# A fixed order for the fp32 weighted sums of grouped heads, and scores against both parts of the keys in one product

## The chip, the cores and the metric

The kernel runs on one core of a Trainium2 chip. The metric is the device time of one execution in microseconds (us), as the median of several runs. TensorE (PE, with its weight loads PEld) multiplies, VectorE (DVE) and ScalarE (ACT) work elementwise, GpSimd (POOL) and SyncE (SP) mostly issue transfers.

## The reference

A decoder trunk of four layers on x of 256 rows by 2048, in fp32. The layers use three kinds of self attention in turn: latent (layers 0 and 3), sparse grouped with a top-k selection of keys (layer 1), and grouped with a sliding window and sinks (layer 2). Every layer also has four memory heads of width 256, which attend to 256 memory rows.

```
h   = rmsnorm(x) ;  q, k, v, mq, gate = split(h @ w_in[i])
s   = q k^T * scale + bias ; masked ; p = softmax(s) ; self = p v      # 32 heads, 4 key groups
sm  = mq mk^T / 16         ;          pm = softmax(sm) ; mem = pm mv   # 4 memory heads
x   = x + (concat(self, mem) * silu(gate)) @ w_out[i]
```

The grouped layers have 32 heads of width 64; eight heads share one of four groups of keys and values. After the last layer a final rmsnorm is applied.

## The kernel before

Matrices are multiplied in fp32r. An fp32 operand is split into a high part (rounded by ACT, line 74) and a low part (the difference, by DVE, line 83), and a product is made of high by high, high by low and low by high. Weights stream from memory through `wr` (SP's queue), are split into `wh` and `wl`, and are multiplied at lines 289 (`rows_by`, output and value weights), 310 and 314 (`columns_by`, queries and gates).

The program is written layer by layer: for each of six parts of a layer (two of memory heads, four of self heads), project, attend, gate, and then the output weights of the part before. A scheduler that simulates the program then places the instructions on each engine, each engine's queue running in order, so that the attention of one part stands among the weight products of others. `tc.keep_in_program_order` pins an instruction behind the pinned ones before it on its engine.

The attention of a grouped layer is `Grouped.attend`, once per group `g` of keys. Its outer loop runs over two halves, the inner one over `odd` in (0, 1), two sets of two heads, 64 queries at a time. For each, `quarter_softmax` takes two of four query quarters `r`; the keys up to the quarter's end count, (r + 1) * 64, or 192 for the last quarter of the windowed layer.

- Scores (line 1033): the queries' high and low parts lie on the 128 partitions, so one product of n keys' high and low parts side by side gives both halves of the score, 2n columns. For the sparse layer's last quarter (n = 256) there are instead two products of 256 columns into the same place (line 1036). `both(r)` tells the two apart.
- Where both halves come apart, DVE adds the bias to the low one (line 601), then adds the high one and takes the minimum (line 603); otherwise line 603 alone adds the bias. ACT takes the exponential (line 605) and normalizes it (line 74).
- PE transposes the weights into `ptp` (line 550), and ACT copies them to `pT`, one tile for each `odd`, in fp32.
- Weighted sums (line 1065): four fp32 products make `o` of 128 partitions by 512 columns. `odd` 0 fills partitions 0 to 63 and uses the array's columns 0 to 63, `odd` 1 the others. For each, keys 0 to 127 (t = 0) give 512 columns and keys 128 to 255 (t = 1) add to the last 256. Their weights are the values, 128 keys by 64. The hardware runs an fp32 product as two passes, which the trace records as two products.
- DVE multiplies `o` by the gate (line 1070), and the result is split into `y` for the output weights.

`memory_attend` does the same for two memory heads of 256. With `both` (layers 0 and 3), lines 652 and 653 make the scores of 128 queries with two products of 512 columns (high queries by both parts of the keys) and two of 256 (low queries by high keys); ACT copies the second half out and DVE adds it while taking the minimum (line 656). Without (layers 1 and 2), line 663 uses six products of 256 columns, and DVE takes the maximum of the sum (line 664).

Of the kernel before, what the change touches and what calls it, by code (L numbers as in the profile page):

```python
# [8 lines left out]
F32 = mybir.dt.float32  # L9
F32R = mybir.dt.float32r  # L10
I32 = mybir.dt.int32
AF = mybir.ActivationFunctionType
OP = mybir.AluOpType
# [32 lines left out]
def kernel(ctx: ExitStack, tc: tile.TileContext, a: dict, out: bass.AP,  # L46
# [536 lines left out]
            normalized(es[b], r[:, b:b + 1], (b + 1) * P)  # L583
        return weights_T(es, [(0, 0), (1, 0), (1, 1)])

    def quarter_softmax(score, bias, first_key, both, b, nsk):

        es = []
        mn, sm = small("mn", 2), small("sm", 2)
        for i, r in enumerate((2 * b, 2 * b + 1)):  # L590
            k0, k1 = first_key(r), (r + 1) * 64
            n = k1 - k0
            sp = score(r, k0, n)
            u = wk.tile([P, S], F32, name="u", tag="e", bufs=4)
            e = wk.tile([P, S], F32, name="e", tag="e", bufs=4) if nsk is None else u
            for z0, z1 in ((0, k0), (k1, (b + 1) * P)):
                if z0 < z1:
                    nc.gpsimd.memset(e[:, z0:z1], 0.0)
            bi, at = bias(r, k0, k1), u[:, k0:k1]
            if both(r):  # L600
                nc.vector.tensor_add(at, sp[:, n:2 * n], bi)
                bi = at
            nc.vector.tensor_tensor_reduce(at, sp[:, :n], bi, -1.0, nsk if nsk is not None else BIG,
                                           op0=OP.add, op1=OP.min, accum_out=mn[:, i:i + 1])
            nc.scalar.activation(e[:, k0:k1], at, AF.Exp, bias=mn[:, i:i + 1], scale=-1.0,
                                 accum_out=sm[:, i:i + 1])
            es.append((e, k0, k1))
        rc = small("rc", 2)
        if nsk is not None:
            d = small("sd", 2)  # L610
            nc.vector.tensor_scalar(d, mn, nsk, None, op0=OP.subtract)
            e2 = small("se", 2)
            nc.scalar.activation(e2, d, AF.Exp)
            s3 = small("sa", 2)
            nc.vector.tensor_add(s3, sm, e2)
            nc.vector.reciprocal(rc, s3)
        else:
            nc.vector.reciprocal(rc, sm)
        for i, (e, k0, k1) in enumerate(es):
            copy_act(e[:, k0:k1], e[:, k0:k1], scale=rc[:, i:i + 1])  # L620
        return weights_T([e for e, _, _ in es], [(i, k) for k in range(b + 1) for i in range(2)])
# [17 lines left out]
            qT.append(q)  # L639
        return nm, kT, v, qT, gate(nm, w, g0 + 2048 + part * 512)  # L640

    def memory_attend(both, nm, kT, v, qT, gT):
        y = act.tile([P, 2, 4, S], F32R, name="y", tag="y", bufs=2)
        for h in range(2):
            es = []
            mn, sm = small("mn", 2), small("sm", 2)
            for b in range(2):
                sp = misc("msp")
                qs = slice(b * P, (b + 1) * P)
                if both:  # L650
                    for k in range(2):
                        nc.tensor.matmul(sp, qT[h][:, 0, k, qs], kT[h][:, :, k, :], start=k == 0, stop=False)
                        nc.tensor.matmul(sp[:, :S], qT[h][:, 1, k, qs], kT[h][:, 0, k, :], start=False, stop=k == 1)
                    s = wk.tile([P, S], F32, name="u", tag="e", bufs=4)
                    copy_act(s, sp[:, S:])
                    nc.vector.tensor_tensor_reduce(s, sp[:, :S], s, -1.0, BIG,
                                                   op0=OP.add, op1=OP.min, accum_out=mn[:, b:b + 1])
                    factor = "neg"
                else:
                    seq = [(qT[h][:, u, k, qs], kT[h][:, v_, k, :])  # L660
                           for k in range(2) for u, v_ in ((0, 0), (0, 1), (1, 0))]
                    for n_, (l, r_) in enumerate(seq):
                        nc.tensor.matmul(sp[:, :S], l, r_, start=n_ == 0, stop=n_ == len(seq) - 1)
                    nc.vector.tensor_reduce(mn[:, b:b + 1], sp[:, :S], AX.X, OP.max, negate=True)
                    s, factor = sp[:, :S], "rstd"
                ms = small("ms", 2)
                nc.vector.tensor_mul(ms[:, :1], mn[:, b:b + 1], nm.col("rstd", b))
                e = wk.tile([P, S], F32, name="e", tag="e", bufs=4)
                nc.scalar.activation(e, s, AF.Exp, bias=ms[:, :1], scale=nm.col(factor, b),
                                     accum_out=sm[:, b:b + 1])  # L670
                es.append(e)
            r = small("rc", 2)
            nc.vector.reciprocal(r, sm)
            for b in range(2):
                normalized(es[b], r[:, b:b + 1], S)
            tp = weights_T(es, [(0, 0), (1, 0), (0, 1), (1, 1)])
            pH, pL = (wk.tile([P, 768], F32R, name="pT", tag="pT", bufs=PT)[:, :512] for z in range(2))
            split(pH, pL, tp)
            o = misc("mo")
            for j in range(2):  # L680
                c = (2 * h + j) * P
                seq = [(v[z][:, t, c:c + P], p_[:, t * S:(t + 1) * S])
                       for t in range(2) for z, p_ in ((0, pH), (0, pL), (1, pH))]
                for n_, (l, r_) in enumerate(seq):
                    nc.tensor.matmul(o[:, j * S:(j + 1) * S], l, r_, start=n_ == 0, stop=n_ == 5)
            gated(y, o, gT, 2 * h)
        return y
# [169 lines left out]
    class Grouped:  # L857
# [164 lines left out]
        def attend(self, g, q, bm, gT):  # L1022
# [3 lines left out]
            for half in range(2):  # L1026
                pT = []
                for odd in range(2):
                    def score(r, k0, n):
                        sp = misc("sp")  # L1030
                        qb = q[half][:, odd, r].rearrange("p j c -> p (j c)")
                        if both(r):
                            nc.tensor.matmul(sp[:, :2 * n], qb, self.k[:, g, :, k0:k0 + n], start=True, stop=True)
                        else:
                            for v in range(2):
                                nc.tensor.matmul(sp[:, :n], qb, self.k[:, g, v, k0:k0 + n],
                                                 start=v == 0, stop=v == 1)
                        return sp

                    def bias(r, k0, k1):  # L1040
                        c0 = (3 - r) * 64
                        bh = bm[:, half * 2 + odd, c0 + k0:c0 + k1]
                        if not self.sparse or r == 0:
                            return bh
                        bs = wk.tile([P, S], F32, name="bs", tag="e", bufs=4)[:, :k1]
                        nc.vector.tensor_add(bs, bh, self.sel[r])
                        return bs

                    def first_key(r):
                        return 64 if r == 3 and not self.sparse else 0  # L1050

                    def both(r):
                        return r < 3 or not self.sparse

                    u0 = g * 4 + half * 2 + odd
                    nsk = None if self.sparse else nsink[:, u0:u0 + 1]
                    pT.append(wk.tile([P, 6, P], F32, name="pT2", tag="pT", bufs=PT))
                    for b in range(2):
                        tp = quarter_softmax(score, bias, first_key, both, b, nsk)
                        i0, i1 = ((0, 2), (2, 6))[b]  # L1060
                        copy_act(pT[odd][:, i0:i1], tp[:, :(i1 - i0) * P].rearrange("p (i c) -> p i c", c=P))
                o = misc("o")
                for t in range(2):
                    for odd in range(2):
                        nc.tensor.matmul(o[64 * odd:64 * odd + 64, t * S:], self.v[:, t, g * 64:g * 64 + 64],
                                         pT[odd][:, 4 * t:4 + 2 * t].rearrange("p i c -> p (i c)"),
                                         start=t == 0, stop=t == 1, tile_position=(0, 64 * odd))
                j = half * 2
                yt = tmp("yt")
                nc.vector.tensor_mul(yt.rearrange("p (j r c) -> p j r c", j=2, r=4),  # L1070
# [148 lines left out]
    for i in range(depth):  # L1219
# [20 lines left out]
        order = [4, 0, 1, 2, 3, 5]  # L1240
        for n_, part in enumerate(order):
            if part >= 4:
                y = memory_attend(kind == 0, *memory_project(nm, i, mixer.w, mixer.mq0, mixer.g0, part - 4,
                                                  mixer.last_of_first()))
            else:
                y = mixer.attend(*mixer.project(part))
            if pending is not None:
                w_out(*pending, False)
            pending = (part, y)
# [62 lines left out]
```

## Time and profile before

| | |
|---|---|
| median of 3 runs | 2571.69 us (2570.69 to 2571.88) |
| the profiled execution, time | 2570.63 us |
| its span, first to last instruction | 2568.9 us |
| granted TensorE clock, mean | 0.999 |
| weighted sums (line 1065), records on PE | 128 |
| scores of memory heads, layers 1 and 2 (line 663) | 96 products |
| the second form of the sparse scores (line 1036) | 32 products |

A row of groups reads: line, engine, operation, tile written and tiles read, shapes, count, then busy us in total and mean ns of one, then the engine's idle time before them and what ended it. A row of the timeline reads: start in us, length in us, engine, line, operation, count. PE's instructions overlap: the next one's start, and not the first one's end, tells when PE went on. A row of the waits says who waited for whom: us in total, times, longest.

### The profile page before, as it was taken

What the parts mean: (1) busy time and instruction counts of PE and PEld (TensorE: products, weight loads), DVE (VectorE), ACT (ScalarE), POOL (GpSimd) and SP (SyncE); (2) the same over time, 40 slices, a digit from 0 to 9 for tenths busy, and PEclk for the clock granted to TensorE, in tenths of its full rate; (3) what the DMA queues carried; (4) which work ended last, traced back from release to release, by engine and by line L of the source; (5) the groups of instructions that cost most, each with busy time, mean ns of one, the idle gap of its engine ahead of it and who ended that gap; (6) DMA issues with size and microseconds to landing.
All of it is one profiled execution on the core that took longest, in us unless ns stands there. A gap on an engine that the chain in (4) does not pass through costs nothing.

```text
span 2568.9 us, 41673 instructions
## 1 busy us (share of the span) xinstructions
PE 2558.5 (100%) x14022; PEld 2186.3 (85%) x14022; DVE 1885.3 (73%) x3800; ACT 1596.3 (62%) x3271; POOL 102.9 (4%) x297
## 2 busy tenths in 40 slices
PE   9999999999999999999999999999999999999998
PEld 8888898888888889888888888888888888888887
DVE  6666667677777687987777777777768767777766
ACT  6556556566566566666666566666656666666655
POOL 1200000000000000000000000000000000000000
PEclk9999999999999999999999999999999999999999
DMA  9888777576677667665666565565555768666765
GB/s 310 262 265 257 238 224 227 165 196 178 183 203 204 185 199 205 197 194 164 185 181 175 170 214 179 165 180 166 176 168 161 238 189 221 190 195 186 222 168 185
DMA packets 478583, 511.68 MB, mean 199 GB/s; under 512 B 70656, under 2 KB 391040, under 8 KB 477728
## 3 DMA queue, kind: packets, MB, share of 16 engines
q1 hardware_dynamic: 461856, 451.82, 59.9%
q0 software_dynamic: 15792, 56.22, 7.0%
q8 instruction: 110, 1.80, 0.3%
q14 instruction: 105, 0.86, 0.1%
q10 hardware_dynamic: 720, 0.98, 0.1%
HBM read 483.67 MB, written 29.46 MB: 200 GB/s over the span
## 4 chain that ended last, share of the span: by engine, by line
PE 98%; DMA 1%; DVE 1%; ACT 0%; issue 0%; SPq 0%; POOL 0%; ACTq 0%; DVEq 0%
PE acc_wo L289 20%; PE acc_g L310 14%; PE acc_g L314 7%; PE acc_mv L289 7%; PE acc_q L310 5%; PE acc_mk L310 5%; PE acc_mq L310 4%; PE acc_cq L310 3%; PE acc_qn L310 3%; PE acc_q L314 2%; PE acc_mk L314 2%; PE acc_mq L314 2%; PE acc_cq L314 2%; PE acc_qr L310 2%; PE acc_qn L314 2%; PE acc_va L289 2%
## 5 line engine op out<-in xcount | busy, mean ns | idle before, releaser
L83 DVE TENSOR_TENSOR wl<-wr,wh 128x512 fp32r<-128x512 f32 (+1 forms) x1712 | 1154.5, 679 | 581.1 <-ACT wh L74 551.5
L74 ACT ACTIVATE wh<-wr 128x512 fp32r<-128x512 f32 (+1 forms) x1712 | 1063.0, 623 | 830.9 <-PE acc_g L310 148.1
L310 PE MATMUL acc_g<-xT,wh 128*128 128x512 f32 x1536 | 483.4, 397 | 0.0
L289 PE MATMUL acc_wo<-wh,y 128*128 128x512 f32 x1504 | 477.1, 392 | 0.0
L289 PEld LDWEIGHTS acc_wo<-wh,y 128*128 128x128 f32 x1504 | 282.5, 188 | 58.9 <-ACT th L531 1.5
L314 PEld LDWEIGHTS acc_g<-xT,wl 128*128 128x128 f32 x1536 | 280.8, 188 | 60.6 <-DVE wl L83 0.5
L314 PE MATMUL acc_g<-xT,wl 128*128 128x256 f32 x1536 | 306.0, 281 | 0.1
L289 PE MATMUL acc_wo<-wl,y 128*128 128x512 f32 x752 | 297.7, 396 | 0.0
L310 PEld LDWEIGHTS acc_g<-xT,wh 128*128 128x128 f32 x1536 | 235.3, 189 | 0.8
L289 PEld LDWEIGHTS acc_wo<-wl,y 128*128 128x128 f32 x752 | 141.4, 188 | 25.9
L310 PE MATMUL acc_q<-xT,wh 128*128 128x512 f32 x512 | 161.3, 396 | 0.0
L310 PE MATMUL acc_mq<-xT,wh 128*128 128x512 f32 x512 | 161.1, 396 | 0.0
L310 PE MATMUL acc_mk<-mT,wh 128*128 128x512 f32 x512 | 160.7, 395 | 0.0
L289 PE MATMUL acc_mv<-wh,mT 128*128 128x512 f32 x512 | 156.8, 390 | 0.2
L310 PE MATMUL acc_qn<-cT,wh 128*128 128x512 f32 x384 | 121.0, 396 | 0.0
L310 PE MATMUL acc_cq<-xT,wh 128*128 128x512 f32 x384 | 120.9, 396 | 0.0
L1231 DVE TENSOR_TENSOR xc<-xc,acc_wo 128x1024 f32<-128x1024 f32 x92 | 112.0, 1218 | 4.2 <-PE acc_wo L289 3.4
L314 PEld LDWEIGHTS acc_mk<-mT,wl 128*128 128x128 f32 x512 | 95.8, 188 | 22.6 <-DVE wl L83 0.2
L289 PEld LDWEIGHTS acc_mv<-wh,mT 128*128 128x128 f32 x512 | 96.3, 188 | 20.7 <-ACT wh L74 0.9
L314 PEld LDWEIGHTS acc_q<-xT,wl 128*128 128x128 f32 x512 | 95.0, 188 | 21.5
L314 PEld LDWEIGHTS acc_mq<-xT,wl 128*128 128x128 f32 x512 | 94.5, 188 | 21.4 <-issue 0.4
L314 PE MATMUL acc_mq<-xT,wl 128*128 128x256 f32 x512 | 101.8, 280 | 0.0
(325 smaller groups left out, 3837.1 us busy)
## 6 DMA issues: line engine op xcount, KB each, us to landing
wr<-in_w_out_dram SPq DMA_DIRECT2D x188, 512.0 KB, 3.7
wr<-in_w_in_a_dram SPq DMA_DIRECT2D x176, 512.0 KB, 4.2
wr<-in_w_mem_kv_dram SPq DMA_DIRECT2D x126, 512.0 KB, 4.8
wr<-in_w_in_b_dram SPq DMA_DIRECT2D x116, 512.0 KB, 3.6
wr<-in_w_in_c_dram SPq DMA_DIRECT2D x104, 512.0 KB, 3.5
wr<-in_w_uq_dram SPq DMA_DIRECT2D x288, 128.0 KB, 2.8
wr<-in_w_in_a_dram SPq DMA_DIRECT2D x32, 288.0 KB, 3.1
mv<-mv POOLq DMA_DIRECT2D x16, 512.0 KB, 6.5
```

The source lines that it names most:

```text
L74: inst = nc.scalar.activation(o, i, AF.Copy, scale=scale)
L83: nc.vector.tensor_sub(lo, src, f32(hi))
L289: nc.tensor.matmul(acc[t][:, :n], q[:, v, (s + k) % 4, t * P:(t + 1) * P], w_[:, :n], start=s + k == 0 and v == 0 and w_ is wh, stop=s + k ...
L310: nc.tensor.matmul(acc[j], wh[:, o:o + P], q[:, :, kt % 4, :], start=kt == 0, stop=False)
L314: nc.tensor.matmul(acc[j][:, 0, :], wl[:, o:o + P], q[:, 0, kt % 4, :], start=False, stop=kt == kts - 1)
L1231: nc.vector.tensor_add(xs, xs, acc)
```

## The change

`quarter_softmax` and `memory_attend` lose their second form, and the four weighted sums of a half are pinned, `odd` 1 ahead of `odd` 0 for each t.

```diff
-            bi, at = bias(r, k0, k1), u[:, k0:k1]
-            if both(r):
-                nc.vector.tensor_add(at, sp[:, n:2 * n], bi)
-                bi = at
-            nc.vector.tensor_tensor_reduce(at, sp[:, :n], bi, -1.0, nsk if nsk is not None else BIG,
+            at = u[:, k0:k1]
+            nc.vector.tensor_add(at, sp[:, n:2 * n], bias(r, k0, k1))
+            nc.vector.tensor_tensor_reduce(at, sp[:, :n], at, -1.0, nsk if nsk is not None else BIG,
...
-                    seq = [(qT[h][:, u, k, qs], kT[h][:, v_, k, :])
-                           for k in range(2) for u, v_ in ((0, 0), (0, 1), (1, 0))]
-                    for n_, (l, r_) in enumerate(seq):
-                        nc.tensor.matmul(sp[:, :S], l, r_, start=n_ == 0, stop=n_ == len(seq) - 1)
-                    nc.vector.tensor_reduce(mn[:, b:b + 1], sp[:, :S], AX.X, OP.max, negate=True)
-                    s, factor = sp[:, :S], "rstd"
+                for k in range(2):
+                    nc.tensor.matmul(sp, qT[h][:, 0, k, qs], kT[h][:, :, k, :], start=k == 0, stop=False)
+                    nc.tensor.matmul(sp[:, :S], qT[h][:, 1, k, qs], kT[h][:, 0, k, :], start=False, stop=k == 1)
+                s = wk.tile([P, S], F32, name="u", tag="e", bufs=4)
+                copy_act(s, sp[:, S:])
+                nc.vector.tensor_tensor_reduce(s, sp[:, :S], s, -1.0, BIG,
...
-                        if both(r):
-                            nc.tensor.matmul(sp[:, :2 * n], qb, self.k[:, g, :, k0:k0 + n], start=True, stop=True)
-                        else:
-                            for v in range(2):
-                                nc.tensor.matmul(sp[:, :n], qb, self.k[:, g, v, k0:k0 + n],
-                                                 start=v == 0, stop=v == 1)
+                        nc.tensor.matmul(sp[:, :2 * n], qb, self.k[:, g, :, k0:k0 + n], start=True, stop=True)
...
                 for t in range(2):
-                    for odd in range(2):
-                        nc.tensor.matmul(o[64 * odd:64 * odd + 64, t * S:], self.v[:, t, g * 64:g * 64 + 64],
+                    for odd in (1, 0):
+                        tc.keep_in_program_order(
+                            nc.tensor.matmul(o[64 * odd:64 * odd + 64, t * S:], self.v[:, t, g * 64:g * 64 + 64],
```

Lines move up by 3 to 18 with it: the scores of memory heads are lines 649 and 650, the grouped scores line 1021, the weighted sums line 1047, and their multiplication by the gate line 1052.

The instructions also move. On PE, layer 1, the first group's first half, where `pT_12586` is the tile of `odd` 0 and `pT_12645` that of `odd` 1, there stands before:

```order
L550 MATMUL ptp<-ident,e 128x128
L1065 MATMUL o<-pT_12586,vs 64x512
L1033 MATMUL sp<-kd,qS 128x128
L1033 MATMUL sp<-kd,qS 128x256
L550 MATMUL ptp<-ident,e 128x128 x3
...
L289 MATMUL acc_wo<-wh,y 128x512
L1065 MATMUL o<-pT_12645,vs 64x512
L1065 MATMUL o<-pT_12586,vs 64x256
L1065 MATMUL o<-pT_12645,vs 64x256
L289 MATMUL acc_wo<-wh,y 128x512
```

and there after the change:

```order
L550 MATMUL ptp<-ident,e 128x128 x4
L289 MATMUL acc_wo<-wl,y 128x512
L289 MATMUL acc_wo<-wh,y 128x512 x2
...
L1047 MATMUL o<-pT_12645,vs 64x512
L1047 MATMUL o<-pT_12586,vs 64x512
L1047 MATMUL o<-pT_12645,vs 64x256
L1047 MATMUL o<-pT_12586,vs 64x256
L1021 MATMUL sp<-kd,qS 128x128
L1021 MATMUL sp<-kd,qS 128x256
```

The product of `odd` 0 with 512 columns has moved from between the transposes, 18 weight products ahead of the others, into one run with them, 12 weight products behind the last transposes. It is so in all 16 halves of the two layers: one product and a run of three before, a run of four now; before, the lone one was followed by scores in eight halves and by transposes in the other eight.

On PE, a little earlier, the first scores of the sparse layer's third and fourth quarters stood like this:

```order
L550 MATMUL ptp<-ident,e 128x128
L1033 MATMUL sp<-kd,qS 128x384
L1036 MATMUL sp<-kd,qS 128x256 x2
L314 MATMUL acc_g<-xT,wl 128x256 x2
L310 MATMUL acc_g<-xT,wh 128x512 x2
```

and now stand like this:

```order
L550 MATMUL ptp<-ident,e 128x128
L1021 MATMUL sp<-kd,qS 128x384
L314 MATMUL acc_g<-xT,wl 128x256 x2
L310 MATMUL acc_g<-xT,wh 128x512 x2
L314 MATMUL acc_g<-xT,wl 128x256 x2
L1021 MATMUL sp<-kd,qS 128x512
L550 MATMUL ptp<-ident,e 128x128
```

The two products of 256 have become one of 512, and some weight products have moved between the two quarters' scores. SP's queue keeps its order, and POOL's differs by where three fills with zeros stand.

More of the change, by code (lines that the diff above doesn't have):

```diff
@@ L584, in masked_softmax, with quarter_softmax @@
         return weights_T(es, [(0, 0), (1, 0), (1, 1)])
-    def quarter_softmax(score, bias, first_key, both, b, nsk):
+    def quarter_softmax(score, bias, first_key, b, nsk):
         es = []
@@ L640, in memory_project, with memory_attend @@
         return nm, kT, v, qT, gate(nm, w, g0 + 2048 + part * 512)
-    def memory_attend(both, nm, kT, v, qT, gT):
+    def memory_attend(nm, kT, v, qT, gT):
         y = act.tile([P, 2, 4, S], F32R, name="y", tag="y", bufs=2)
@@ L649, in memory_attend @@
                 qs = slice(b * P, (b + 1) * P)
[L650 to L658, printed above, removed]
-                else:
-                    seq = [(qT[h][:, u, k, qs], kT[h][:, v_, k, :])
-                           for k in range(2) for u, v_ in ((0, 0), (0, 1), (1, 0))]
-                    for n_, (l, r_) in enumerate(seq):
-                        nc.tensor.matmul(sp[:, :S], l, r_, start=n_ == 0, stop=n_ == len(seq) - 1)
-                    nc.vector.tensor_reduce(mn[:, b:b + 1], sp[:, :S], AX.X, OP.max, negate=True)
-                    s, factor = sp[:, :S], "rstd"
+                for k in range(2):
[4 more added lines that the diff above has]
+                nc.vector.tensor_tensor_reduce(s, sp[:, :S], s, -1.0, BIG,
+                                               op0=OP.add, op1=OP.min, accum_out=mn[:, b:b + 1])
                 ms = small("ms", 2)
@@ L668, in memory_attend @@
                 e = wk.tile([P, S], F32, name="e", tag="e", bufs=4)
-                nc.scalar.activation(e, s, AF.Exp, bias=ms[:, :1], scale=nm.col(factor, b),
+                nc.scalar.activation(e, s, AF.Exp, bias=ms[:, :1], scale=nm.col("neg", b),
                                      accum_out=sm[:, b:b + 1])
@@ L1031, in score @@
                         qb = q[half][:, odd, r].rearrange("p j c -> p (j c)")
-                        if both(r):
-                            nc.tensor.matmul(sp[:, :2 * n], qb, self.k[:, g, :, k0:k0 + n], start=True, stop=True)
-                        else:
-                            for v in range(2):
-                                nc.tensor.matmul(sp[:, :n], qb, self.k[:, g, v, k0:k0 + n],
-                                                 start=v == 0, stop=v == 1)
+                        nc.tensor.matmul(sp[:, :2 * n], qb, self.k[:, g, :, k0:k0 + n], start=True, stop=True)
                         return sp
@@ L1050, in first_key @@
                         return 64 if r == 3 and not self.sparse else 0
-                    def both(r):
-                        return r < 3 or not self.sparse
                     u0 = g * 4 + half * 2 + odd
@@ L1058, in attend @@
                     for b in range(2):
-                        tp = quarter_softmax(score, bias, first_key, both, b, nsk)
+                        tp = quarter_softmax(score, bias, first_key, b, nsk)
                         i0, i1 = ((0, 2), (2, 6))[b]
@@ L1063, in attend @@
                 for t in range(2):
-                    for odd in range(2):
-                        nc.tensor.matmul(o[64 * odd:64 * odd + 64, t * S:], self.v[:, t, g * 64:g * 64 + 64],
-                                         pT[odd][:, 4 * t:4 + 2 * t].rearrange("p i c -> p (i c)"),
-                                         start=t == 0, stop=t == 1, tile_position=(0, 64 * odd))
+                    for odd in (1, 0):
+                        tc.keep_in_program_order(
+                            nc.tensor.matmul(o[64 * odd:64 * odd + 64, t * S:], self.v[:, t, g * 64:g * 64 + 64],
+                                             pT[odd][:, 4 * t:4 + 2 * t].rearrange("p i c -> p (i c)"),
+                                             start=t == 0, stop=t == 1, tile_position=(0, 64 * odd)))
                 j = half * 2
@@ L1242 @@
             if part >= 4:
-                y = memory_attend(kind == 0, *memory_project(nm, i, mixer.w, mixer.mq0, mixer.g0, part - 4,
+                y = memory_attend(*memory_project(nm, i, mixer.w, mixer.mq0, mixer.g0, part - 4,
                                                   mixer.last_of_first()))
```

## The prediction

> **What bounds the kernel now.** I read the page of the profiled execution first: the busy times of part 1, then the chain that ended last in part 4.
>
> ```profile
> PE 2558.5 (100%) x14022; PEld 2186.3 (85%) x14022; DVE 1885.3 (73%) x3800; ACT 1596.3 (62%) x3271; POOL 102.9 (4%) x297
> ...
> PE 98%; DMA 1%; DVE 1%; ACT 0%; issue 0%; SPq 0%; POOL 0%; ACTq 0%; DVEq 0%
> ```
>
> TensorE (PE) is busy for 2558.5 of 2568.9 us, and 98% of the last chain is its own work. So the kernel costs what its products cost, one behind the other, unless PE is made to wait. The change touches layers 1 and 2 alone, so I looked next at a stretch of layer 1's attention (the windows view: busy time and count of each engine, then the granted clock), and at whom PE waited for in the whole program (the waits view: total us, times, longest).
>
> ```profile
> 1100.00:1400.00 300.00, 300.00 (x1594) 243.56 (x1593) 228.81 (x518) 200.96 (x452) 12.03 (x44) 1.00 0.61 179
> ```
>
> ```profile
> PE msp L663 <- DMA mkr<-mkT: 0.6, 1, 0.6
> ```
>
> In these 300 us PE is never free, at the full clock (1.00), while VectorE (DVE) has 71 us to spare and ScalarE (ACT) 99 us. Apart from the program's first product, the only wait that the view puts on PE is 0.6 us for a memory key tile. An edit is therefore worth what it does to PE's queue; work on the other engines is free as long as it comes in time.
>
> **The weighted sums.** A busy PE is made of overlapping durations here, so I don't use means of one instruction; I use the distance from one start to the next, which adds up to the span. The groups view says what the sums are: 32 products of 512 columns, each run as two passes (64 records), and as many of 256.
>
> ```profile
> L1065 PE MATMUL o<-pT,vs 128*64 128x512 f32 x64 | 34.3, 618 | 0.0
> ```
>
> In the order before, each of the 16 halves (2 layers, 4 groups, 2 halves) has one early product alone and a later run of three. The timeline of PE (start, length, line) shows an early one between a transpose and a pair of scores, and below it the same pair without it.
>
> ```profile
> 1123.22 0.27 PE L550 MATMUL ptp<-ident,e 128*128 128x128 f32 x1
> 1123.42 1.07 PE L1065 MATMUL o<-pT,vs 128*64 128x512 f32 x2
> 1124.42 0.50 PE L1033 MATMUL sp<-kd,qS 128*128 128x128 f32 x2
> 1124.76 0.49 PE L550 MATMUL ptp<-ident,e 128*128 128x128 f32 x3
> ```
>
> ```profile
> 1110.74 0.27 PE L550 MATMUL ptp<-ident,e 128*128 128x128 f32 x1
> 1110.77 0.48 PE L1033 MATMUL sp<-kd,qS 128*128 128x128 f32 x2
> 1111.09 0.49 PE L550 MATMUL ptp<-ident,e 128*128 128x128 f32 x3
> ```
>
> From the transpose to the next transposes it is 1.54 us with the early product (1124.76 - 1123.22) and 0.35 us without (1111.09 - 1110.74): it costs 1.19 us. Only 1.00 us lies between its own start and the next one's; the rest is the delay of the product before it and of the one behind it. In eight of the 16 halves the neighbours are scores as here; in the other eight a run of transposes is cut in two:
>
> ```profile
> 1153.38 0.27 PE L550 MATMUL ptp<-ident,e 128*128 128x128 f32 x1
> 1153.59 1.07 PE L1065 MATMUL o<-pT,vs 128*64 128x512 f32 x2
> 1154.59 0.55 PE L550 MATMUL ptp<-ident,e 128*128 128x128 f32 x3
> 1154.89 0.49 PE L314 MATMUL acc_q<-xT,wl 128*128 128x256 f32 x2
> ```
>
> ```profile
> 1087.06 0.60 PE L550 MATMUL ptp<-ident,e 128*128 128x128 f32 x4
> 1087.41 0.48 PE L314 MATMUL acc_q<-xT,wl 128*128 128x256 f32 x2
> ```
>
> That is 1.51 us against 0.35 us for four transposes in one run, so 1.16 us. Both kinds together: 8 x 1.19 + 8 x 1.16 = 18.8 us of PE time go to products that stand alone.
>
> The run of three shows what such a product costs in company. First PE, then its weight loads (PEld), then the groups of PE in the 0.06 us from 1128.80 on:
>
> ```profile
> 1128.53 0.39 PE L289 MATMUL acc_wo<-wh,y 128*128 128x512 f32 x1
> 1128.84 1.50 PE L1065 MATMUL o<-pT,vs 128*64 128x512 f32 x6
> 1130.28 0.50 PE L289 MATMUL acc_wo<-wh,y 128*128 128x512 f32 x1
> ```
>
> ```profile
> 1128.84 0.20 PEld L1065 LDWEIGHTS o<-pT,vs 128*64 128x64 f32 x4 [0.35 <-ACT e L74]
> 1129.33 0.14 PEld L1065 LDWEIGHTS o<-pT,vs 128*64 128x64 f32 x1 [0.29 <-issue]
> 1129.75 0.14 PEld L1065 LDWEIGHTS o<-pT,vs 128*64 128x64 f32 x1 [0.29 <-issue]
> 1130.28 0.19 PEld L289 LDWEIGHTS acc_wo<-wh,y 128*128 128x128 f32 x1 [0.39 <-ACT th L531]
> ```
>
> ```profile
> L1065 PE MATMUL o<-pT,vs 128*64 128x512 f32 x1 | 0.6, 643 | 0.0
> L1065 PE MATMUL o<-pT,vs 128*64 128x256 f32 x1 | 0.4, 430 | 0.0
> ```
>
> The six passes take 1.44 us (1130.28 - 1128.84). They are: two passes of 512 columns for odd head, t = 0; two of 256 for the even head, t = 1; two of 256 for the odd head, t = 1. In the first 0.02 us after 1128.84 a pass of 512 and one of 256 have both begun: the two heads use different 64 columns of the array and run side by side. The single loads at 1129.33 and 1129.75 stand where the odd head's second long pass and its first short pass begin (a load is issued when the one before it has gone into use), so the odd head alone accounts for all of it: 0.49 + 0.42 + 0.53 us. The even head's two short passes cost nothing.
>
> After the change the four products stand in one run: odd 512, even 512, odd 256, even 256. If each head keeps to its own 64 columns as in the trio, the odd head still takes 1.44 us and the even head the same, begun 0.01 us later: 1.45 us. This cannot be under 1.44 us, which one head needs; it is over that if the two share something that 0.45 us of common work did not show. With no sharing at all it would be 0.49 + 3 x 0.42 + 4 x 0.21 + 0.11 = 2.70 us, where 0.21 us is a short pass (half of 0.42) and 0.11 us what is left of 0.53 us for the end of the run. I take 1.45 us, the value nearest to the trio's row. The early products' 18.8 us then go, and 16 x 0.01 = 0.2 us come.
>
> **The scores.** For the sparse layer's fourth quarter the change makes two products of 256 columns into one of 512; in the memory heads six of 256 into two of 512 and two of 256.
>
> ```profile
> 1103.15 0.42 PE L1033 MATMUL sp<-kd,qS 128*128 128x384 f32 x1
> 1103.40 0.40 PE L1036 MATMUL sp<-kd,qS 128*128 128x256 f32 x2
> 1103.64 0.40 PE L314 MATMUL acc_g<-xT,wl 128*128 128x256 f32 x2
> ```
>
> ```profile
> 2505.17 0.39 PE L652 MATMUL msp<-mkr,mqT 128*128 128x512 f32 x1
> 2505.40 0.28 PE L653 MATMUL msp<-mkr,mqT 128*128 128x256 f32 x1
> 2505.52 0.40 PE L314 MATMUL acc_g<-xT,wl 128*128 128x256 f32 x2
> ```
>
> ```profile
> 1527.71 0.71 PE msp L663 x6
> ```
>
> Two products of 256 took 0.24 us (1103.64 - 1103.40), one of 512 in layer 3 took 0.23 us: 16 x 0.01 = 0.2 us less. Six of 256 took 0.71 us (a row of the chain in order of time); a 512 and a 256 took 0.35 us, twice 0.70 us: 16 x 0.01 = 0.2 us less. The columns that PE streams are the same, so nothing more is to be had there; the number of instructions does not bound it.
>
> What is added stands on other engines: 16 additions on DVE in the sparse layer, and 16 copies on ACT in the memory heads, whose reduction keeps its length. The nearest rows of the same shapes:
>
> ```profile
> L571 DVE TENSOR_TENSOR u<-sp,caus 128x256 f32<-128x256 f32 x32 | 13.3, 417 | 0.0
> L74 ACT ACTIVATE u<-msp 128x256 f32<-128x256 f32 x16 | 6.0, 377 | 6.9 <-PE msp L653 6.9
> ```
>
> That is 16 x 0.417 = 6.7 us of DVE and 16 x 0.377 = 6.0 us of ACT. I cost both at nothing: PE's products of the gate and output weights cover them, and DVE and ACT have 71 and 99 us free in 300. If that cover were gone in full, it would be 12.7 us. They also lengthen the way from a score to its transpose by 0.4 us. For a quarter pair in the trace, the normalized weights are ready well before the transpose at 1110.74 needs them:
>
> ```profile
> 1108.60 0.84 ACT L74 ACTIVATE e<-e,rc 128x192 f32<-128x192 f32 x2
> ```
>
> Ready at 1109.44, used at 1110.74: 1.30 us in hand, of which 0.42 us would be used.
>
> **The re-planned order.** The scheduler places everything around these products anew, which no row prices. From below I allow 2 us (the 0.6 us wait and similar small ones could go), from above 3 us (0.2 us at each of 16 halves, half of one added DVE step). I take nothing.
>
> **The sum**, against the profiled execution: its span is 2568.9 us, its time 2570.63 us, 1.7 us outside the span. PE's queue changes by -18.8 + 0.2 - 0.2 - 0.2 = -19.0 us, so the span becomes 2549.9 us and the time 2551.6 us. The median of the three runs is 1.1 us above the profiled one: 2552.7 us.
>
> **Rivals.**
>
> *Passes start in the program's order.* If the two passes of one product must start before those of the next, the order is odd long, odd long, even long, even long, odd short, odd short, even short, even short, and a pass overlaps only its neighbour of the other head. With the durations above: odd 0 to 0.49 and to 0.91, even from 0.49 to 0.91 and to 1.33, odd short from 0.91 to 1.12 and to 1.33, even short to 1.54 and 1.75, and 0.11 at the end: 1.86 us. That is 0.41 us more in 16 halves, 6.6 us: 2559.3 us. Against it stands the trio, where a pass of 256 (the even head's) begins within 0.02 us of the first pass of 512, ahead of that product's own second pass. The Trainium skill, page "TensorE: Matmul & The Clock Gate", section "Part 3: Packing small matmuls", says that products start and end strictly in program order with no reordering; by that rule this rival would hold, and the trio's records already speak against it for the passes of one fp32 product.
>
> *No overlap of two long products.* The trio only shows a short pass beside a long one. If two streams of 512 columns into one PSUM bank take turns, a run costs 2.70 us, 1.25 us more than forecast in each half, 20.0 us in all: 2572.7 us, the same as before.
>
> *PE held at the fixed run.* The run now begins with the head that is finished last, and pinned in a queue that runs in order: whatever stands behind it on PE (output weights, the next scores) waits for the copy of that head's weights on ACT. At the trio the copy is early:
>
> ```profile
> 1125.29 0.60 ACT L74 ACTIVATE pT<-ptp 128x512 f32<-128x512 f32 x1 [1.93 <-PE ptp L550]
> ```
>
> Done at 1125.89, used at 1128.84: 2.95 us in hand. If the copy came that much later against PE, each further us would cost 16 us; the gain is gone at 1.2 us of waiting per half, and the kernel slower by over 0.2% (5.1 us, about what a measurement here tells from no change) at 1.5 us. With 2 us of waiting it is 2552.7 + 32 = 2584.7 us. For it speaks that all is planned anew: in the place shown above, 12 products of the output weights stand between the last transposes and the run, where 18 stood before. Against it: twelve at 0.23 us (the row of 2505.17) are 2.8 us, and the copy above was done 1.1 us after the transposes at 1124.76 began, so some 1.7 us would still be in hand.
>
> **Chances.** The forecast has 0.82, since both its terms are start-to-start distances that repeat in all 16 halves and the side-by-side passes are seen. Program order has 0.09, no overlap 0.05, PE held 0.04. The forecast's own range is 2550.7 to 2555.7 us (the re-planning's bounds). It holds 0.82; a little is kept for errors of reading the rows, and the range is carried on to the nearest rival, 2550.0 to 2560.0 us. Faster by over 0.2%: 0.82 + 0.09 = 0.91; within 0.2%: 0.05; slower: 0.04.
>
> **What would show it.** In the profile of the changed kernel: the weighted sums in 16 runs of eight passes, each 1.45 us from its first start to the next line's; both 512-column passes begun within 0.02 us; PE busy near 2539.5 us and still some 100% of the span; no new wait of PE for a copy of the weights; DVE's busy time up by 7 us and ACT's by 6 us. A run of 1.86 or 2.70 us shows one of the first two rivals. A PE that waits in front of the sums, or for scores and transposes, by more than 3 us in all would make the forecast wrong.

## The result, and the profile after the change

| | before | after |
|---|---|---|
| median, measured in turn on one chip (6 runs each) | 2571.28 us (2570.51 to 2571.88) | 2555.14 us (2553.34 to 2556.49) |
| ratio, with its 95% interval | | 0.9938 (0.9925 to 0.9951) |
| the profiled execution, time | 2570.63 us | 2553.34 us |
| its span | 2568.9 us | 2551.4 us |

The kernel is faster by 16.1 us at the median; the forecast was 2552.7 us, so it falls 2.4 us short of it, inside the range. The runs also lie further apart than those of before: 3.2 us from lowest to highest, against 1.4 us. Both points are taken up below.

The page of after begins, and its chain of work ends, with these lines:

```profile
PE 2538.6 (99%) x13974; PEld 2179.4 (85%) x13974; DVE 1891.8 (74%) x3832; ACT 1604.7 (63%) x3287; POOL 102.6 (4%) x297
...
PE 98%; DMA 1%; DVE 0%; ACT 0%; issue 0%; SPq 0%; POOL 0%; DVEq 0%
```

PE's busy time fell by 19.9 us and it still carries 98% of the chain. DVE's went up by 6.5 us and ACT's by 8.4 us, and the chain's shares of both are no larger than before.

The timeline of PE at the first run of weighted sums (start, length, line, operation, count), the place where before showed the run of three:

```profile
1128.51 0.61 PE L289 MATMUL acc_wo<-wh,y 128*128 128x512 f32 x2
1129.05 1.51 PE L1047 MATMUL o<-pT,vs 128*64 128x512 f32 x8
1130.49 0.50 PE L1021 MATMUL sp<-kd,qS 128*128 128x128 f32 x2
```

All eight passes stand together and PE goes on after 1.44 us (1130.49 - 1129.05), the time that six took before. The groups of PE in the 0.08 us from 1129.00 on say how that is possible:

```profile
L1047 PE MATMUL o<-pT,vs 128*64 128x512 f32 x2 | 0.7, 643 | 0.0
```

Two passes of 512 columns began within 0.03 us of the run's start at 1129.05. They cannot both be of one head: a head's second long pass came 0.49 us after its first in the run of three. The two heads' long passes run side by side. It is the same in all 16 halves: eight passes each, 1.44 us from the first start to the next line's.

What the waits view puts on PE (total us, times, longest) is longer than the two rows of before (the program's first product, 1.1 us in both, is left out):

```profile
PE acc_g L310 <- DVE mqT L352: 1.9, 1, 1.9
PE acc_mv L289 <- ACT wh L74: 1.2, 2, 1.0
...
PE msp L649 <- DMA mkr<-mkT: 0.6, 1, 0.6
```

Two of them are new. The wait of `acc_mv` stands at the program's start and costs nothing against before: at 1000 us, ahead of everything that the change touches, the two programs are level within 0.04 us. The wait of `acc_g` does cost: once, for 1.9 us, a product of the gate (line 310) waits for the low part of the memory heads' queries (line 352 in `head_parts`). To see when the time was won and lost, take the same product in both traces at the ends of the regions. First before, then after: the first product of layer 2's keys and values, the first of layer 3's keys, and the first of the last output weights (each cut off one timeline).

```profile
1483.42 0.39 PE L289 MATMUL acc_kv<-wh,xT 128*128 128x512 f32 x1
...
1966.23 0.29 PE L289 MATMUL acc_kva<-wh,xT 128*128 128x288 f32 x1
...
2515.26 0.40 PE L289 MATMUL acc_wo<-wh,y 128*128 128x512 f32 x1
```

```profile
1473.89 0.39 PE L289 MATMUL acc_kv<-wh,xT 128*128 128x512 f32 x1
...
1949.49 0.29 PE L289 MATMUL acc_kva<-wh,xT 128*128 128x288 f32 x1
...
2498.20 0.40 PE L289 MATMUL acc_wo<-wh,y 128*128 128x512 f32 x1
```

After layer 1 the changed kernel is 9.5 us ahead (eight halves, so 1.19 us each), after layer 2 only 16.7 us, at the end 17.1 us. Layer 1 gave what its eight halves were to give; layer 2 gave 7.2 us, some 2 us too little. The wait stands in layer 2. PE there, DVE below it, then ACT:

```profile
1871.65 1.51 PE L1047 MATMUL o<-pT,vs 128*64 128x512 f32 x8
1873.09 0.73 PE L649 MATMUL msp<-mkr,mqT 128*128 128x512 f32 x2
1875.74 0.50 PE L310 MATMUL acc_g<-xT,wh 128*128 128x512 f32 x1 [1.92 <-DVE mqT L352]
```

```profile
1873.21 0.69 DVE L1052 TENSOR_TENSOR yt<-o,gT 128x512 f32<-128x512 f32 x1 [0.33 <-PE o L1047]
1873.81 1.28 DVE L351 TENSOR_TENSOR zl<-acc_mq,mqT 128x512 f32<-128x512 f32 x2
1875.01 0.68 DVE L352 TENSOR_TENSOR mqT<-zl,acc_mq 128x512 fp32r<-128x512 f32 x1
```

```profile
1859.87 0.58 ACT L74 ACTIVATE mqT<-acc_mq 128x512 fp32r<-128x512 f32 x1
```

Read it backwards. The gate's first product needs an accumulator, and both (`acc` is a ring of two) still hold the queries of the two memory heads. The first comes free when DVE has taken its low part (lines 351 and 352). ACT had written the high part, which line 351 subtracts, by 1860.45, so line 351 could have run 13 us earlier. But on DVE it stands behind line 1052, which multiplies the last weighted sums by the gate, and that waits for the run of four at 1871.65. In `before` the three stood in the same order on DVE; there the last run stood earlier among the queries' products:

```profile
1885.24 1.50 PE L1065 MATMUL o<-pT,vs 128*64 128x512 f32 x6
1886.67 0.39 PE L314 MATMUL acc_mq<-xT,wl 128*128 128x256 f32 x1
...
1891.21 0.63 PE L310 MATMUL acc_mq<-xT,wh 128*128 128x512 f32 x2
1891.67 1.11 PE L663 MATMUL msp<-mkr,mqT 128*128 128x256 f32 x8
1892.62 0.63 PE L310 MATMUL acc_g<-xT,wh 128*128 128x512 f32 x2
```

From 1886.67 to 1892.62 PE had 6 us of products to do while DVE took the low part. After the change the queries' products are done before the run, and 0.73 us of scores are all that stands between it and the gate.

### The profile page after: what moved, and what is told of

Its sections match the earlier page's. It is cut to its first block, busy times and chain, and to the rows that moved or that the text cites. A ratio compares the mean times of both kernels' runs of the same rounds, so it can differ in the third digit from the quotient of the medians.

```text
span 2551.4 us, 41632 instructions
## 1 busy us (share of the span) xinstructions
PE 2538.6 (99%) x13974; PEld 2179.4 (85%) x13974; DVE 1891.8 (74%) x3832; ACT 1604.7 (63%) x3287; POOL 102.6 (4%) x297
## 4 chain that ended last, share of the span: by engine, by line
PE 98%; DMA 1%; DVE 0%; ACT 0%; issue 0%; SPq 0%; POOL 0%; DVEq 0%
PE acc_wo L289 20%; PE acc_g L310 14%; PE acc_g L314 7%; PE acc_mv L289 7%; PE acc_q L310 5%; PE acc_mk L310 5%; PE acc_mq L310 4%; PE acc_cq L310 4%; PE acc_qn L310 4%; PE acc_q L314 2%; PE acc_mk L314 2%; PE acc_mq L314 2%; PE acc_cq L314 2%; PE acc_qr L310 2%; PE acc_qn L314 2%; PE acc_va L289 2%
## 5 line engine op out<-in xcount | busy, mean ns | idle before, releaser
L314 PE MATMUL acc_q<-xT,wl 128*128 128x256 f32 x512 | 102.1, 281 | 0.0
```

What stands on the lines that cost most here:

```text
L314: nc.tensor.matmul(acc[j][:, 0, :], wl[:, o:o + P], q[:, 0, kt % 4, :], start=False, stop=kt == kts - 1)
```

## The experiments

The theory that the nine kernels below were to test: the whole gain is that of the lone early product, which the fixed order brings into the company of the other three, where the two heads' passes run side by side; and the shortfall is the wait of layer 2, made by DVE's queue. The rivals: that the scores carry part of the gain; that it rests on the order of the passes in the run; that the two heads' sharing of the array has nothing to do with it; that the shortfall comes from somewhere else. All ratios are to the kernel before, measured in turn on the same chip, with their 95% intervals.

### The scores alone

After the change, with the weighted sums as they were:

```diff
-                    for odd in (1, 0):
-                        tc.keep_in_program_order(
-                            nc.tensor.matmul(o[64 * odd:64 * odd + 64, t * S:], self.v[:, t, g * 64:g * 64 + 64],
+                    for odd in range(2):
+                        nc.tensor.matmul(o[64 * odd:64 * odd + 64, t * S:], self.v[:, t, g * 64:g * 64 + 64],
```

> The full change with the order of the weighted sums left to the scheduler, as before; the scores all take the one-product form. Theory: PE streams the same columns, so 0.3 us less than the kernel before, at most 1 us either way, with one lone product and a run of three in each half again. Rival (fewer products and loads are what is gained): 5 us or more faster than before. Second rival (the added 6.7 us of DVE and 6.0 us of ACT come in the way): 3 to 13 us slower than before.

Measured: 2571.27 us (2570.49 to 2572.32) against 2571.34, ratio 1.000 (0.9991 to 1.0009). The lone product is back in PE's timeline:

```profile
1126.54 1.07 PE L1046 MATMUL o<-pT,vs 128*64 128x512 f32 x2
1127.54 0.50 PE L1021 MATMUL sp<-kd,qS 128*128 128x128 f32 x2
```

The new scores are worth nothing that can be measured, within 2.3 us either way, although they take 48 instructions off PE and add 32 to DVE (16 additions, and 16 short reads of an accumulator that the new reduction of the memory scores brings) and 16 to ACT. The additions are as free as they were costed.

### The order alone

The kernel before, with the pinned order and nothing else:

```diff
-                    for odd in range(2):
-                        nc.tensor.matmul(o[64 * odd:64 * odd + 64, t * S:], self.v[:, t, g * 64:g * 64 + 64],
+                    for odd in (1, 0):
+                        tc.keep_in_program_order(
+                            nc.tensor.matmul(o[64 * odd:64 * odd + 64, t * S:], self.v[:, t, g * 64:g * 64 + 64],
```

> The kernel before with the fixed order of the weighted sums alone; the scores keep both forms. Theory (the gain is products that no longer stand alone): 16 runs of 8 passes of 1.44 us, 18.8 us of PE time gone, and the 1.9 us wait in front of the gate's first product in layer 2 is there too, since here too the last run stands right ahead of it: 16 to 17 us under the kernel before, the same as the full change within 1 us. Rival (the one-product scores bring part of the gain): at least 5 us slower than the full change.

Measured: 2556.88 us (2555.09 to 2557.40), ratio 0.9943 (0.9930 to 0.9955). That is 14.5 us, under the 16 to 17 that were expected, and 1.7 us above the full change by the medians; but the intervals of the two ratios overlap, and the full change with its loops exchanged (the next kernel), on the same chip, lies only 0.8 us lower. So the order brings the gain, to within what these runs can tell. The waits of PE hold the same row as in after, so the wait of layer 2 comes with the order too, and not with the scores:

```profile
PE acc_g L310 <- DVE mqT L352: 1.9, 1, 1.9
```

### One head after the other

After, with the loops exchanged: all of odd 1, then all of odd 0.

```diff
-                for t in range(2):
-                    for odd in (1, 0):
+                for odd in (1, 0):
+                    for t in range(2):
```

> The full change with the four sums of a half pinned head by head: odd 512, odd 256, even 512, even 256. Theory (each half of the array's columns works through its own products, whatever stands between them): the first pass of the even head begins within 0.03 us of the odd head's first, a run takes 1.44 us, and the time is that of the full change. Rival (passes start in the program's order): the even head begins when the odd head's last pass has begun, 1.12 us late, a run takes 2.56 us, and 16 x 1.12 = 18 us are lost: the time of the kernel before.

Measured: 2556.06 us (2554.23 to 2557.55), ratio 0.9940 (0.9928 to 0.9952), no different from after. PE's timeline, and below it the groups of PE in the 0.09 us from 1129.95 on:

```profile
1129.99 1.52 PE L1047 MATMUL o<-pT,vs 128*64 128x512 f32 x8
1131.44 0.33 PE L1021 MATMUL sp<-kd,qS 128*128 128x128 f32 x1
```

```profile
L1047 PE MATMUL o<-pT,vs 128*64 128x512 f32 x2 | 0.7, 644 | 0.0
```

The run takes 1.45 us in this order as well. Here the even head's first pass stands behind four passes of the odd head, and still it begins within 0.05 us of the odd head's first. By the starts in the trace it is 13 ns (13 or 14 in all 16 runs), against 7 ns in after, where two passes stand ahead of it. So passes do not start in the program's order where they use different columns of the array. The Trainium skill, page "TensorE: Matmul & The Clock Gate", section "Part 3: Packing small matmuls — row/col tiling", says that products start and end strictly in program order; these records do not agree with it for the starts of the passes of fp32 products, and here the measurement decides (the ends are not measured).

### Even head first

After, pinned in the other order:

```diff
-                    for odd in (1, 0):
+                    for odd in range(2):
```

> The full change with the four sums pinned in the old order of the heads: even before odd for each t. Theory (a pin only fixes who is first; the even head's weights are ready 5 us before the odd head's, so the scheduler again lets its long product go ahead alone, and the odd head's first place is what keeps the run together): one lone product and a run of three in each half, the time of the kernel before within 1.5 us. Rival (the pin itself keeps the four together, in either order): 16 runs of 1.44 us and 15 us or more under the kernel before.

Measured: 2572.30 us (2571.50 to 2575.16), ratio 1.0004 (0.9994 to 1.0014): no gain at all. Pinning alone does not bring the products together: all 16 halves have one lone product and a run of three again. The even head's weights are ready first, and the scheduler places its product ahead of the others:

```profile
1126.41 0.60 PE L550 MATMUL ptp<-ident,e 128*128 128x128 f32 x4
1126.94 1.07 PE L1047 MATMUL o<-pT,vs 128*64 128x512 f32 x2
1127.94 0.49 PE L1021 MATMUL sp<-kd,qS 128*128 128x128 f32 x2
```

With the head that is finished last in front, nothing of the run can stand earlier. The order of the two heads does its work in the plan, and not on the array.

### Both heads in one half of the array

After, with both heads' weights in columns 64 to 127 and a sum of its own for each. The even head's sums are multiplied by the odd head's gate rows, so this kernel leaves out the even head's own gate, and DVE multiplies once more per half.

```diff
-                o = misc("o")
+                o2 = [misc("o"), misc("o")]
...
-                            nc.tensor.matmul(o[64 * odd:64 * odd + 64, t * S:], self.v[:, t, g * 64:g * 64 + 64],
-                                             start=t == 0, stop=t == 1, tile_position=(0, 64 * odd)))
+                            nc.tensor.matmul(o2[odd][64:, t * S:], self.v[:, t, g * 64:g * 64 + 64],
+                                             start=t == 0, stop=t == 1, tile_position=(0, 64)))
```

> The full change, but both heads of a weighted sum use the same 64 columns of the array (the upper ones) and write two tiles; the even head's sums are gated with the odd head's gate rows, by a second multiplication on DVE. Theory (what hides the even head is that it has 64 columns of its own): the eight passes stand one behind the other, a run takes 2.70 us instead of 1.44, and 16 x 1.26 = 20 us come back: 2573 to 2578 us, the time of the kernel before or a little over it. Rival (products overlap in a run whatever columns they use): a run stays under 2 us and the time under 2566 us.

Measured: 2579.52 us (2578.29 to 2579.94), ratio 1.0030 (1.0018 to 1.0042). On the same chip after itself took 2555.41 us, so this is 24.1 us slower. PE's timeline, and the groups of PE in the 0.5 us from 1129.40 on:

```profile
1129.50 2.79 PE L1047 MATMUL o<-pT,vs 128*64 128x512 f32 x8
1132.22 0.33 PE L1021 MATMUL sp<-kd,qS 128*128 128x128 f32 x1
```

```profile
L1047 PE MATMUL o<-pT,vs 128*64 128x512 f32 x1 | 0.6, 643 | 0.0
```

The same eight passes take 2.72 us, in each of the 16 halves, and 0.4 us after the first no other has begun: they run one behind the other. The prediction had worked out 2.70 us for no sharing. Of the 24.1 us, 16 x 1.28 = 20.5 are the runs. The other 3.6 us take it past the 2573 to 2578 us that were expected. Two waits of PE are here that after doesn't have:

```profile
PE acc_wo L289 <- ACT wh L74: 1.1, 2, 0.5
PE o L1047 <- ACT pT L74: 1.0, 1, 1.0
```

But others are shorter: all waits of PE in the view come to 7.2 us here and to 6.5 us in after on the same chip (the next section's profile), so waits make up only 0.7 us, and what the rest is stays open. That the heads use different columns is what makes the run cheap.

### The changed kernel once more

After unchanged, on the chip on which the kernel above and the last two below (`e6_sums_zl`, `e7_early_keys`) ran.

> The full change once more, as the measure for the others of this group and for what differs from one execution to the next. Theory: the same 16 runs of 1.44 us and the same 1.9 us wait for the low part of the memory queries; what else differs in the span are waits for transfers, at the start and for the memory keys of layer 2. 2553 to 2557 us.

Measured: 2555.41 us (2554.29 to 2556.51), ratio 0.9937 (0.9925 to 0.9950). Its profiled execution was the slowest of its five, where the first profile had caught the fastest of its six: a span of 2554.6 us against 2551.4. The wait of layer 2 is 1.9 us in both. What differs stands right behind it. The windows view (busy time and count of each engine, granted clock, then transfers) for some 4.3 us after the wait, first of the first profile, then of this one:

```profile
1875.70:1880.00 4.30, 4.26 (x24) 3.73 (x25) 2.56 (x4) 1.26 (x2) 0.00 (x0) 1.00 0.07 12
```

```profile
1877.35:1881.60 4.25, 4.21 (x14) 3.61 (x15) 1.87 (x3) 0.63 (x1) 0.00 (x0) 0.60 0.02 4
```

At the full clock PE did 24 products; here 14, at a mean granted clock of 0.60. The first 14 took 4.21 us, against 2.67 us. The rows of PE that show it, from this profile and then from the first:

```profile
1877.39 0.78 PE L310 MATMUL acc_g<-xT,wh 128*128 128x512 f32 x2 [1.92 <-DVE mqT L352]
...
1881.60 0.28 PE L314 MATMUL acc_g<-xT,wl 128*128 128x256 f32 x1
```

```profile
1875.74 0.73 PE L310 MATMUL acc_g<-xT,wh 128*128 128x512 f32 x2 [1.92 <-DVE mqT L352]
...
1878.41 0.40 PE L314 MATMUL acc_g<-xT,wl 128*128 128x256 f32 x2
```

So the wait costs 1.9 us, and behind it 1.5 us more where the clock falls. Two other waits were longer too:

```profile
PE acc_mv L289 <- ACT wh L74: 2.1, 3, 1.2
...
PE msp L649 <- DMA mkr<-mkT: 1.4, 1, 1.4
```

With 0.9 us more for `wh` (2.1 against 1.2) and 0.8 us more for the memory key (1.4 against 0.6) that is the whole difference of 3.2 us between the two spans. Such a difference from one execution to the next widens the spread of the runs; which of the unprofiled runs had the lower clock can't be seen (the mean clock on record is 0.999 for all five, the profiled one included).

### A buffer of its own for the low part

Why does line 351 stand behind line 1052 on DVE? Both write a tile of one ring of four buffers (`tmp`), and the theory is that a ring hands its buffers out in the order of the program, in which the gated sum comes first. So the edit to after takes the low part of the memory queries in layers 1 and 2 from another ring (`part_tile`):

```diff
-    def head_parts(dst, pair):
+    def head_parts(dst, pair, own=False):
...
-        z = tmp("zl").rearrange("p (j c) -> p j c", j=2)
+        z = (part_tile(F32)[:] if own else tmp("zl")).rearrange("p (j c) -> p j c", j=2)
...
-            head_parts(q, acc)
+            head_parts(q, acc, i in (1, 2))
```

> The full change, and in layers 1 and 2 the difference that gives the low part of the memory queries is written to another pool's buffer, so that its place in the ring is not behind that of the gated sum. Theory (the low part stood behind the last gated sum on DVE because both draw on one ring of four buffers, and PE waited 1.9 us for the accumulator that it frees): no wait of PE at the gate's first product, 2 us less than the full change, 18 to 19 us under the kernel before. Rival (PE waits there because DVE is late with other work): the wait stays, or another of the same length comes in its place, and the time is that of the full change within 0.5 us.

Measured: 2553.15 us (2551.88 to 2554.87), ratio 0.9930 (0.9918 to 0.9943). DVE now takes the low part at 1862.22, 11.6 us earlier than in after, and on PE the gate's products stand ahead of the last run of weighted sums:

```profile
1862.22 0.68 DVE L351 TENSOR_TENSOR hl<-acc_mq,mqT 128x512 f32<-128x512 f32 x1
...
1863.62 0.68 DVE L352 TENSOR_TENSOR mqT<-hl,acc_mq 128x512 fp32r<-128x512 f32 x1
```

```profile
1873.17 0.62 PE L310 MATMUL acc_g<-xT,wh 128*128 128x512 f32 x2
...
1875.13 1.51 PE L1047 MATMUL o<-pT,vs 128*64 128x512 f32 x8
```

The wait is gone from the view. By the medians the edit gives some 2 us, though its interval and that of after, which was not measured in turn with it, overlap; what is certain is the row that went. The same edit to the kernel with the order alone:

> The fixed order of the weighted sums alone (no change of the scores), with the low part of the memory queries in another pool's buffer. Theory: no wait at the gate's first product, and the scores' form is worth 0.3 us: the time of the full change with that buffer, within 1 us, 18 us under the kernel before. Rival (the score form matters once the wait is gone): at least 2 us away from it.

Measured: 2552.74 us (2552.11 to 2553.80), ratio 0.9926 (0.9913 to 0.9940), against 0.9943 without it. The wait is gone there as well, and the scores make no difference with it either. This kernel ran on the chip of after taken again, and there the gain is clear of the spread: 2552.11 to 2553.80 us with the buffer, 2554.29 to 2556.51 in after, which lacks the buffer (and has the new scores, which are worth nothing measurable).

### Memory keys of layer 2 loaded earlier

The longest single wait that was left, for a memory key in layer 2, was 1.5 us in the first of these two profiles. Its load is held back on POOL behind an instruction of the layer (`behind`). The edit, on top of the last one to after, lifts that for layer 2:

```diff
-        if part == 0:
+        if part == 0 and i != 2:
             not_before(behind)
```

> The full change with the low part of the memory queries in another pool's buffer, and in layer 2 the loads of memory keys and values are not held back until the layer's own keys are there. Theory (PE's wait of 0.6 to 1.9 us in front of the first memory scores of layer 2 is a load that was issued late): that wait goes, 1 to 1.5 us less than without it, 19 to 20 us under the kernel before. Rival (the load then takes bandwidth or buffers from what is streamed at that time): another wait of a us or more, no gain.

Measured: 2550.94 us (2550.61 to 2551.47), ratio 0.9920 (0.9906 to 0.9934): 20.8 us faster than before, a little more than was expected, and the fastest and steadiest of all versions. PE's waits are down to these:

```profile
PE acc_mv L289 <- ACT wh L74: 1.4, 3, 0.9
PE wu L122 <- DVE ones L116: 1.1, 1, 1.1
```

## Why the prediction was right, and where it was off

**What bounds the kernel.** Right. PE stayed the bound, and the time followed its queue.

**The lone early products, -18.8 us.** Right. The order alone carries the gain, as far as the runs can tell (14.5 of 16.1 us, with overlapping intervals), and layer 1's region, with eight of them, ended 9.5 us earlier.

**The run of four, 1.45 us.** Right: 1.44 us in after, 1.45 us with one head after the other. The reason was right too: in one half of the array the same passes take 2.72 us.

**The scores, -0.4 us.** Nothing that a measurement can tell, as forecast; the experiment alone can't tell -0.4 from 0.

**DVE and ACT, at nothing.** Right in what it says of the time. DVE's busy time went up by 6.5 us, where 6.7 had been worked out, and there luck helped: the sum has 16 additions but not the 16 reads of an accumulator that came with the memory heads' reduction, 0.083 us each, 1.3 us in all. ACT's went up by 8.4 us in place of 6.0. The copies themselves are as costed, 16 more at the median length below; the other 2.4 us are little more than two executions of after differ by (1604.7 and 1606.5 us):

```profile
L74 ACT ACTIVATE u<-msp x32: 360/383/388, 472.5 to 2488.7; 128x256 f32<-128x256 f32 x32
```

**The re-planned order, "I take nothing".** This is the term that was off. It cost 1.9 us in layer 2 (2.3 us in the kernel with both heads in one half), at one place, in all kernels with the order and the shared ring, and in some executions 1.5 us more by the lower clock behind it. The bounds of -2 to +3 us held it; the value taken did not. The rows that would have shown it were in the trace of before: DVE's queue there already had the low part of the memory queries behind the last gated sum, with only PE's 6 us of query products as cover, and the order of the changed program showed the last run behind these products.

**The rivals.** That passes start in the program's order fell with the exchanged loops. That two long products don't overlap fell with the two starts within 0.03 us and the run of 1.44 us. That PE is held at the fixed run for the copy of the weights did not happen: no wait of after names `pT`. But what is behind the new wait is of its kind: something that queues behind the fixed run and for which PE then waits. It came once and not 16 times, through DVE's queue and an accumulator, and so it cost 2 us and not 32.

**The sum.** Of the profiled span -19.0 us were forecast and -17.5 measured. The wait, +1.9 us, more than makes up the difference; the 0.4 us left over are no more than what waits for loads differ by from one execution to the next (0.6 and 1.4 us for the same memory key in two profiles of after). At the median the forecast was 2552.7 us, and the versions without the wait measured 2553.15 and 2552.74 us. A smaller term was off too: the sum took 1.7 us of time outside the span, from before, whose other runs have 1.7 to 1.9 us. The six runs of after have 1.9 to 3.1 us, 2.15 at the middle, so some 0.4 of the 2.4 us by which the median falls short lie there. No run shows what they are.

## What to carry to other kernels

Price a small instruction in the engine's queue by the distance between its neighbours with it and without it, and look for a place where it costs nothing beside others. When a step is pinned to come later, list what stands behind its consumers on the other engines, above all what shares a ring of buffers with them, and what the bound engine has left to do in that time. A planner that hands out buffers in the program's order can hold back a step that has been ready for 13 us.

## What the runs showed of the hardware

The granted clock of TensorE fell after a wait of only 1.9 us, in a program that otherwise keeps it at 0.999. It did so in the profile of after taken again (0.60 over the 4.25 us behind the wait) and not in the first one (1.00), at the same place and with the same wait. Two other kernels divide in the same way, in the 4.25 us behind the same wait. First one head after the other, then the order alone:

```profile
1878.15:1882.40 4.25, 4.25 (x15) 3.65 (x16) 1.84 (x3) 0.63 (x1) 0.00 (x0) 0.60 0.02 4
```

```profile
1877.33:1881.58 4.25, 4.25 (x24) 3.72 (x25) 2.24 (x4) 1.26 (x2) 0.00 (x0) 1.00 0.07 11
```

The kernel with both heads in one half waited 2.3 us there, and its clock fell too (0.60 over the 4.23 us behind the wait). The length of a wait does not decide it alone: in one head after the other PE also waited 1.94 us for a memory key, up to 1517.01 us, and behind that wait the clock stayed full:

```profile
1516.90:1521.10 4.20, 4.09 (x23) 3.65 (x24) 1.30 (x2) 1.38 (x3) 0.00 (x0) 1.00 0.91 319
```

The Trainium skill, page "TensorE: Matmul & The Clock Gate", section "Part 1: The HAM clock gate (the "warmup" mystery)", describes a free-running window of 3413 ns over which the array's activity is judged; that a window can or cannot fall on the wait would fit a drop in some executions only. Its advice to avoid gaps of over some 3.4 us is not strict enough here. No run set out to vary the length of the wait or the work ahead of it, so where the bound lies, and what part that work has in it, stays open.

A head's passes need not wait for those that stand ahead of them on PE: with one head's four passes issued first, the other head's began within 0.05 us of their start, and the run took 1.45 us. Two long streams side by side cost no time that shows (eight passes take 1.44 us, as the run of three took for six); the same passes in one half take 1.9 times as long (2.72 us against 1.44).
